# One operand tile of the FFN's seven-product loop placed 64 bytes further on

## The chip, the cores and the metric

The kernel runs on one core of one Trainium2 chip. The metric is the device time of one execution in microseconds (us): the median over runs.

## The reference, cut to what matters

Two layers of a streaming encoder over 512 positions of 1024 channels. Each layer has a mixing half (three attention-like branches, merged and projected) and a feed-forward half. The change lies in the feed-forward half:

```python
u = rms_norm(x, g_ffn[l]) * (1 + sc_f) + sh_f
h = jax.nn.silu(u @ w_ffn_gate[l]) * (u @ w_ffn_up[l])
x = x + gt_f * (h @ w_ffn_down[l])
```

The hidden width is 2816, that is 22 blocks of 128 hidden channels, in each of two layers.

## The kernel before, in words

Activations are held transposed: 128 channels on the partitions, 512 positions along the free dimension. Every float32 product is made of three fp32r matmuls (`mm3`, lines 225 to 227): with a matrix split into a high part and a low remainder, high times high (L225), weights high times activations low (L226), weights low times activations high (L227). In a matmul of the trace, `y<-t4h,wh` means: into `y`, moving operand (activations) `t4h`, stationary operand (weights) `wh`.

In the feed-forward half, the first three hidden blocks are computed plainly. For the other 19, gate and up are the two rows of a 2x2 block product over (half of the 1024 channels) x (half of the 512 positions), made with seven half-size products instead of eight. Four sums of weights are made for each block (`sums`: DVE L1011, POOL L1012 and L1013; `s31` and `s24` hold two each) and split by ACT and DVE (L269, L270); four differences of activations are made once for each layer and split by `divided` (lines 960 to 970: `t1` to `t4`, each a high and a low tile of 128 x 4 x 256 fp32r). Each product is four channel blocks times three matmuls, 12 matmuls of 256 columns.

The order on TensorE is as written in the loop over `f`. In one round, seen from the third product, TensorE does:

| product | into | weights | activations |
|---|---|---|---|
| t3 | y of block f | s31, first half | t3 |
| v | v of block f | s24, second half | uh/ul (the input itself) |
| z | z of block f+1 | a12 | uh/ul |
| t4 | y of block f | wh/wl, second half | t4 |
| t2 | y of block f+1 | s24, first half | t2 |
| t1 | v of block f+1 | s31, second half | t1 |
| y-u | y of block f+2 | wh/wl, first half | uh/ul |

After t2, ACT copies the half-made `y` out of PSUM (`kept_copy`, L1031), and t3 may not add to that bank before the copy is done. ACT's order around it is: cast of `s24h`, copy of `y` behind t2, copy of `v` behind t1, copy of the next `y`. The tiles `s31h`, `s31l` have one buffer: their next contents are cast (ACT L269) once t3, their last reader, has read them. Each engine runs its instructions in the program's order.

Where the tiles lie in a partition, as an offset into a line of 128 bytes: `uh`, `ul`, `wh`, `wl` and `t1` to `t4` begin at 0; `a12`, `s31` and `s24` begin at 64, since the pool that holds them ends with a tile of 16 floats (`half`, line 1092) and grows downwards from the pool of `t1` to `t4`. Of the seven products, y-u and t4 have both operands at 0; the other five have activations at 0 and weights at 64.

Of the kernel before, what the change touches and what calls it, by code (L numbers as in the profile page):

```python
# [8 lines left out]
F32 = mybir.dt.float32  # L9
# [8 lines left out]
P = 128  # L18
# [50 lines left out]
def tile_hybrid_trunk(ctx: ExitStack, tc: tile.TileContext, xT, cvec, pos, cst, cmask, vec, gfin,  # L69
# [14 lines left out]
    def scoped(name, side=None):  # L84
        return tc.tile_pool(name=name, bufs=1, side=side, reuse_waits="tile")
# [3 lines left out]
    def pst(tag, name):  # L89
        return ps.tile([P, S], F32, tag=tag, bufs=PB[tag], name=name)  # L90
# [112 lines left out]
    def W(unit, n=1, raw=3, ready=2, lag=0):  # L203

        i = at[0]
        if fourth[0]:
            raw, ready = 4, 3
        assert LOADS[i][0] == unit, (LOADS[i][0], unit)
        at[0] = i + n
        divide(i + n)  # L210

        def ahead():
            divide(i + max(n, ready + 1))
            fetch(i + max(n, raw + 1))

        if lag:
            later(lag, ahead)
        else:
            ahead()
        return splits[i] if n == 1 else splits[i : i + n]  # L220
# [8 lines left out]
    def gemm(o, wt, acts, m=P, start=True, stop=True, c0=0, cols=FULL):  # L229

        wh, wl = wt
        n = len(acts)
        for k, (ah, al) in enumerate(acts):
            cs = slice(c0 + k * m, c0 + (k + 1) * m)
            mm3(o, wh[:, cs], wl[:, cs], ah[:, cols], al[:, cols], start and k == 0, stop and k == n - 1)
            if k < n - 1:
                yield
# [25 lines left out]
    def run(g):  # L263
        for _ in g:
            tick()

    def split(h, l, src, scale=None):
        if scale is None:
            act.copy(h, src)  # L269
            dve.tensor_sub(l, src, h.bitcast(F32))  # L270
        else:
            act.activation(h, src, AF.Copy, scale=scale)
            dve.scalar_tensor_tensor(l, src, scale, h.bitcast(F32), ALU.mult, ALU.subtract)
# [240 lines left out]
    for l in range(L):  # L514
# [396 lines left out]
        tp = tp_.enter_context(scoped(f"st{l}", "right"))  # L911
# [16 lines left out]
        def gated(f, t, t2):  # L928
            g = tp.tile([P, S], F32, tag="g", bufs=3, name="g")
            fn(g, t, AF.Silu)  # L930
            dve.tensor_mul(g, g, t2)
            kept(f, g)
# [25 lines left out]
        def divided(name, src):  # L958
            h, lo = (tp.tile([P, 4, H], F32R, name=f"{name}{a}") for a in "hl")
            split(h, lo, src)  # L960
            TB[name] = [(h[:, k], lo[:, k]) for k in range(4)]
# [5 lines left out]
        pool.tensor_sub(b12, b22, b12)  # L967
        divided("t3", b12)
        dve.scalar_tensor_tensor(b21, b11, -1.0, b21, ALU.mult, ALU.subtract)
        divided("t4", b21)  # L970
        for f in range(1, NSTD):
            if f == 1:
                t = ts[2]
            else:
                t = pst("mm", "fg")
                run(gemm(t, W(("gu", l, 2 * f)), us))
            t2 = pst("s", "fu")
            run(gemm(t2, W(("gu", l, 2 * f + 1)), us))
            gated(f, t, t2)
# [281 lines left out]
def _build(arrays):  # L1261
    import concourse.bacc as bacc

    nc = bacc.Bacc("TRN2", target_bir_lowering=False, num_devices=1)
    feeds, args = {}, []
    for name, a in arrays.items():
        feeds[f"in_{name}_dram"] = a
        args.append(nc.dram_tensor(f"in_{name}_dram", a.shape, mybir.dt.from_np(a.dtype), kind="ExternalInput").ap())
    args.append(nc.dram_tensor("out_dram", (KC, P, S), F32, kind="ExternalOutput").ap())
    with tile.TileContext(nc) as tc:  # L1270
        tile_hybrid_trunk(tc, *args)
    return nc, feeds
# [10 lines left out]
```

## Time and profile before

| | |
|---|---|
| median of 3 runs | 1820.93 us (1818.77 to 1822.38) |
| the profiled execution's own time | 1820.55 us |
| its span (first to last instruction) | 1818.8 us |
| PE busy | 1783.5 us, 98% of the span |
| DVE busy | 1390.3 us, 76% |
| ACT busy | 956.8 us, 53% |
| mean granted TensorE clock | 0.997 of full speed |

PE is TensorE's matmuls, PEld its weight loads, which run beside the matmuls. Matmuls are pipelined, so the recorded length of one (0.28 us) is longer than the step from one start to the next; how long a product holds TensorE is read from the start of its first matmul to the start of the next product's first. In rows of the timeline the columns are: start in us from the span's start, length in us, engine, line, operation, out<-in, shape, count, and in brackets the idle time before it and what ended it.

### The profile page before, as it was taken

The page shows a single profiled execution, that of the slowest core. Times are in us where ns is not written, and L with a number is a line of the kernel's source. Part 1 is how long each engine was busy: PE and PEld are TensorE (multiplying, and loading weights), DVE is VectorE, ACT ScalarE, POOL GpSimd, SP SyncE. Part 2 cuts the span into 40 slices and gives each one's busy share as a digit, 9 for nine tenths or more (in the row PEclk, how much of TensorE's full clock was granted, in tenths as well). Part 3 has the DMA queues.
Part 4 walks back from the last instruction along what each step waited for, and adds up shares of the span by engine and source line. Part 5 has one row for each costly group of instructions (what it writes and reads, how often), then busy time and mean ns, then how long its engine had stood idle before and what let it go on. Part 6 is the DMA issues. An engine that isn't in the chain of part 4 may idle for free.

```text
span 1818.8 us, 27810 instructions
## 1 busy us (share of the span) xinstructions
PE 1783.5 (98%) x10324; PEld 1547.5 (85%) x10324; DVE 1390.3 (76%) x2317; ACT 956.8 (53%) x1735; POOL 258.9 (14%) x390
## 2 busy tenths in 40 slices
PE   8999999999999999999999999999999999999997
PEld 6788788888889899988887887888888889999887
DVE  8889887777668888967558898877776588898533
ACT  5667874453436555552257688645443374555531
POOL 0212100001000333300003121000110013232000
PEclk9999999999999999999999999999999999999999
DMA  8423324334654444468634223333365434445631
GB/s 338 110 67 85 88 76 122 121 113 133 214 162 151 129 133 145 128 218 272 209 119 103 61 69 88 104 122 115 117 201 171 149 93 122 140 136 163 215 96 46
DMA packets 86263, 247.52 MB, mean 136 GB/s; under 512 B 11824, under 2 KB 15024, under 8 KB 86128
## 3 DMA queue, kind: packets, MB, share of 16 engines
q1 hardware_dynamic: 75120, 224.83, 40.1%
q0 software_dynamic: 11008, 20.92, 4.0%
q8 instruction: 81, 1.33, 0.3%
q14 instruction: 54, 0.44, 0.1%
HBM read 220.74 MB, written 15.73 MB: 130 GB/s over the span
## 4 chain that ended last, share of the span: by engine, by line
PE 83%; DVE 7%; ACT 4%; issue 3%; DMA 2%; POOL 1%; DVEq 0%; SPq 0%; POOLq 0%; ACTq 0%
PE gate L225 5%; PE gate L227 5%; PE gate L226 5%; PE proj L225 5%; PE proj L226 4%; PE dn L226 4%; PE dn L227 4%; PE dn L225 4%; PE proj L227 4%; PE y L225 3%; PE y L227 3%; PE y L226 3%; PE o L225 2%; PE o L227 2%; PE o L226 2%
## 5 line engine op out<-in xcount | busy, mean ns | idle before, releaser
L196 ACT CAST wh<-wraw 128x1024 fp32r<-128x1024 f32 (+4 forms) x316 | 294.1, 934 | 312.4 <-PE dn L226 76.6
L198 DVE TENSOR_TENSOR wl<-wraw,wh 128x1024 fp32r<-128x1024 f32 (+4 forms) x316 | 361.1, 1146 | 116.1 <-ACT wh L196 110.2
L225 PE MATMUL proj<-uh,wh 128*128 128x512 f32 x384 | 161.1, 419 | 0.2
L225 PE MATMUL gate<-uh,wh 128*128 128x512 f32 x384 | 153.4, 400 | 0.0
L226 PE MATMUL proj<-ul,wh 128*128 128x512 f32 x384 | 151.2, 394 | 0.0
L227 PE MATMUL proj<-uh,wl 128*128 128x512 f32 x384 | 151.1, 393 | 0.0
L227 PE MATMUL gate<-uh,wl 128*128 128x512 f32 x384 | 150.2, 391 | 0.0
L226 PE MATMUL gate<-ul,wh 128*128 128x512 f32 x384 | 150.2, 391 | 0.0
L225 PE MATMUL dn<-wh 128*128 128x512 f32 (+1 forms) x396 | 145.1, 366 | 0.0
L226 PE MATMUL dn<-wl,wh 128*128 128x512 f32 (+1 forms) x396 | 144.9, 366 | 0.0
L227 PE MATMUL dn<-wh,wl 128*128 128x512 f32 (+1 forms) x396 | 144.7, 365 | 0.0
L395 DVE CUSTOM_DVE_ANT_0 wraw<-wraw,condb 128x1024 f32<-128x1024 f32 x80 | 97.6, 1220 | 56.9 <-DMA wraw<-in_w_ada_dram 56.7
L227 PEld LDWEIGHTS proj<-uh,wl 128*128 128x128 f32 x384 | 72.3, 188 | 16.7
L226 PEld LDWEIGHTS dn<-wl,wh 128*128 128x128 f32 x396 | 74.7, 189 | 12.8 <-DVE wl L198 0.7
L227 PEld LDWEIGHTS gate<-uh,wl 128*128 128x128 f32 x384 | 72.1, 188 | 15.8
L225 PEld LDWEIGHTS dn<-wh 128*128 128x128 f32 x396 | 74.7, 189 | 12.1
L227 PEld LDWEIGHTS dn<-wh,wl 128*128 128x128 f32 x396 | 74.7, 189 | 11.9
L225 PEld LDWEIGHTS gate<-uh,wh 128*128 128x128 f32 x384 | 72.2, 188 | 12.9
L1012 POOL TENSOR_TENSOR s<-s,wraw 128x512 f32<-128x512 f32 x38 | 49.2, 1295 | 239.0 <-ACT a12h L269 209.7
L226 PEld LDWEIGHTS gate<-ul,wh 128*128 128x128 f32 x384 | 72.3, 188 | 12.5
L106 ACT ACTIVATE lefts<-ss 128x512 f32<-128x512 f32 (+1 forms) x64 | 28.0, 438 | 100.0 <-DVE ss L446 84.4
L225 PEld LDWEIGHTS proj<-uh,wh 128*128 128x128 f32 x384 | 72.6, 189 | 9.0 <-PE sm L742 0.8
(440 smaller groups left out, 5314.7 us busy)
## 6 DMA issues: line engine op xcount, KB each, us to landing
wraw<-in_w_proj_dram SPq DMA_DIRECT2D x96, 512.0 KB, 3.8
wraw<-in_w_gu_dram SPq DMA_DIRECT2D x88, 512.0 KB, 4.2
wraw<-in_w_ada_dram SPq DMA_DIRECT2D x80, 512.0 KB, 3.6
wraw<-in_w_dn_dram SPq DMA_DIRECT2D x32, 512.0 KB, 4.0
wraw<-in_w_o_dram SPq DMA_DIRECT2D x48, 256.0 KB, 2.6
h_kept<-g POOLq DMA_DIRECT2D x44, 256.0 KB, 5.1
wraw<-h_kept SPq DMA_DIRECT2D x22, 512.0 KB, 5.0
wada<-in_w_ada_dram SPq DMA_DIRECT2D x16, 512.0 KB, 6.0
```

The costliest lines, as they stand in the source:

```text
L106: i = act.activation(*args, **kw).ins
L196: ins = [act.copy(wh[:, :c], raws[j][:, :c]).ins]
L198: ins.append(dve.tensor_sub(wl[:, :c], raws[j][:, :c], wh[:, :c].bitcast(F32)).ins)
L225: pe.matmul(o, wh, ah, start=start, stop=False, skip_group_check=again)
L226: pe.matmul(o, wh, al, start=False, stop=False, skip_group_check=again)
L227: pe.matmul(o, wl, ah, start=False, stop=stop, skip_group_check=again)
L395: ins = dve.tensor_tensor_reduce(out=wt, in0=wt, in1=condb, op0=ALU.mult, op1=ALU.add, scale=1.0, scalar=0.0, accum_out=m).ins
L1012: pool.tensor_add(s24[:, 0], s31[:, 1], ra[:, :HC])
```

## The change

Two tiles that nothing reads or writes are allocated around the fourth difference: 64 bytes before it and 192 bytes behind, in the pool that holds `t1` to `t4`.

```diff
         divided("t3", b12)
         dve.scalar_tensor_tensor(b21, b11, -1.0, b21, ALU.mult, ALU.subtract)
+        tp.tile([P, 16], F32, name="half0")
         divided("t4", b21)
+        tp.tile([P, 48], F32, name="half1")
         for f in range(1, NSTD):
```

No instruction is added, and on each engine they stand in the order of before; only addresses move. Of the seven products' operands (byte in the partition, and offset in a line of 128):

| tile | before | after |
|---|---|---|
| t3h | 212736 (0) | 212480 (0) |
| t4h | 220928 (0) | 220736 (64) |
| t4l | 225024 (0) | 224832 (64) |
| s31h | 177856 (64) | 177600 (64) |
| wh, three buffers in turn | 77056, 81152, 85248 (0) | the same |
| uh of the first channel block | 27904 (0) | the same |

The whole right-hand stack of the feed-forward half (`uf`, `g`, `t1` to `t3`, and `a12`, `s31`, `s24`, the copies) moves down by 256 bytes, which leaves its offset in a line as it was. In the table of products, t4 is the only row whose operands' distance changes: activations at 64, weights at 0. A few later instructions wait for one semaphore more, since a tile that follows there now overlaps another old one: of those on ACT, in each layer one cast of a kept h block waits for the second-last store of h besides the last.

## Rows read from the trace of the kernel before

**Rows 1.** The page: busy time by engine, and the engines' shares of the chain that ended last.
```profile
PE 1783.5 (98%) x10324; PEld 1547.5 (85%) x10324; DVE 1390.3 (76%) x2317; ACT 956.8 (53%) x1735; POOL 258.9 (14%) x390
...
PE 83%; DVE 7%; ACT 4%; issue 3%; DMA 2%; POOL 1%; DVEq 0%; SPq 0%; POOLq 0%; ACTq 0%
```
**Rows 2.** Groups of PE instructions, shapes kept apart: busy us, mean ns of one, idle before. One group of each kind of product (152 matmuls = 38 rounds x 4).
```profile
L225 PE MATMUL y<-uh,wh 128*128 128x256 f32 x152 | 43.0, 283 | 0.0
...
L225 PE MATMUL y<-t4h,wh 128*128 128x256 f32 x152 | 42.9, 282 | 0.0
L225 PE MATMUL y<-t3h,s31h 128*128 128x256 f32 x152 | 42.8, 282 | 5.2 <-ACT y L1031 5.0
L225 PE MATMUL z<-uh,a12h 128*128 128x256 f32 x152 | 42.3, 278 | 0.0
...
L225 PE MATMUL v<-t1h,s31h 128*128 128x256 f32 x152 | 42.0, 276 | 0.0
```
**Rows 3.** Timeline of PE in the middle of the first layer's loop: the first matmul of each product, over two rounds (from t3 to t3 to t3).
```profile
636.36 0.28 PE L225 MATMUL y<-t3h,s31h 128*128 128x256 f32 x1
...
637.76 0.28 PE L225 MATMUL v<-uh,s24h 128*128 128x256 f32 x1
...
639.18 0.28 PE L225 MATMUL z<-uh,a12h 128*128 128x256 f32 x1
...
640.59 0.28 PE L225 MATMUL y<-t4h,wh 128*128 128x256 f32 x1
...
642.02 0.28 PE L225 MATMUL y<-t2h,s24h 128*128 128x256 f32 x1
...
643.38 0.28 PE L225 MATMUL v<-t1h,s31h 128*128 128x256 f32 x1
...
644.74 0.28 PE L225 MATMUL y<-uh,wh 128*128 128x256 f32 x1
...
646.18 0.28 PE L225 MATMUL y<-t3h,s31h 128*128 128x256 f32 x1
...
647.54 0.28 PE L225 MATMUL v<-uh,s24h 128*128 128x256 f32 x1
...
648.90 0.28 PE L225 MATMUL z<-uh,a12h 128*128 128x256 f32 x1
...
650.26 0.28 PE L225 MATMUL y<-t4h,wh 128*128 128x256 f32 x1
...
651.70 0.28 PE L225 MATMUL y<-t2h,s24h 128*128 128x256 f32 x1
...
653.06 0.28 PE L225 MATMUL v<-t1h,s31h 128*128 128x256 f32 x1
...
654.42 0.28 PE L225 MATMUL y<-uh,wh 128*128 128x256 f32 x1
...
655.86 0.28 PE L225 MATMUL y<-t3h,s31h 128*128 128x256 f32 x1
```
**Rows 4.** Timeline of PE at the start of the same loop (the products t2, t1 and y-u, and the loop's first t3), and its last t3 but one.
```profile
609.85 0.30 PE L225 MATMUL y<-t2h,s24h 128*128 128x256 f32 x1
...
611.29 0.28 PE L225 MATMUL v<-t1h,s31h 128*128 128x256 f32 x1
...
612.70 0.28 PE L225 MATMUL y<-uh,wh 128*128 128x256 f32 x1
...
616.74 0.39 PE L225 MATMUL y<-t3h,s31h 128*128 128x256 f32 x1 [2.43 <-ACT y L1031]
...
783.07 0.39 PE L225 MATMUL y<-t3h,s31h 128*128 128x256 f32 x1 [0.19 <-ACT y L1031]
```
**Rows 5.** Timeline of all engines in the second of the two rounds of rows 3: the work on the weights' sums and the copy that t3 waits for.
```profile
645.54 0.36 ACT L1031 COPY y<-y 128x256 f32<-128x256 f32 x1
...
647.32 0.28 PE L226 MATMUL y<-t3l,s31h 128*128 128x256 f32 x1
...
647.68 1.05 ACT L269 CAST s31h<-s 128x1024 fp32r<-128x1024 f32 x1 [0.89 <-PE y L226]
...
648.77 1.22 DVE L270 TENSOR_TENSOR s31l<-s,s31h 128x1024 fp32r<-128x1024 f32 x1 [0.54 <-ACT s31h L269]
...
649.91 0.42 DVE L1083 TENSOR_TENSOR g<-v,y 128x256 f32<-128x256 f32 x1
...
650.36 0.63 ACT L106 ACTIVATE g<-g 128x512 f32<-128x512 f32 x1 [1.62 <-DVE g L1083]
...
650.90 0.61 ACT L269 CAST a12h<-wraw 128x512 fp32r<-128x512 f32 x1
...
651.61 1.29 POOL L1012 TENSOR_TENSOR s<-s,wraw 128x512 f32<-128x512 f32 x1 [6.55 <-ACT a12h L269]
...
652.98 1.37 POOL L1013 TENSOR_TENSOR s<-s,wraw 128x512 f32<-128x512 f32 x1
...
654.38 1.05 ACT L269 CAST s24h<-s 128x1024 fp32r<-128x1024 f32 x1 [1.55 <-POOL s L1013]
655.34 0.36 ACT L1031 COPY y<-y 128x256 f32<-128x256 f32 x1
```
**Rows 6.** Timeline of PE at the end of the same loop: the last t1, then the last t3 (no y-u stands between them there), the last t4 and the first matmul behind the loop.
```profile
790.21 0.28 PE L225 MATMUL v<-t1h,s31h 128*128 128x256 f32 x1
...
791.57 0.28 PE L225 MATMUL y<-t3h,s31h 128*128 128x256 f32 x1
...
794.29 0.28 PE L225 MATMUL y<-t4h,wh 128*128 128x256 f32 x1
...
795.73 0.40 PE L225 MATMUL dn<-wh 128*128 128x512 f32 x1
```

## The prediction, made before the changed kernel ran

> **What bounds the kernel now.** First the page's busy times and its chain: TensorE is busy for 98% of the span and holds 83% of the chain that ended last [rows 1]. So a step saved between matmuls counts, unless TensorE then waits for somebody. Next the groups by shape: in the loop of seven products the matmuls with both operands at offset 0 have a recorded mean of 283 and 282 ns, those 64 bytes apart 276, 278 or 282 [rows 2]. Recorded lengths of pipelined matmuls overlap, so the price is read from the starts in the timeline [rows 3], product by product, 12 matmuls each. The reader is to see three paces there:
>
> - y-u and t4, operands at the same offset: 1.44 us in the second round (644.74 to 646.18, and 650.26 to 651.70), 0.120 us a matmul.
> - Products 64 bytes apart, fast: 1.36 us, 0.113 a matmul (t2, t1 in both rounds; t3, v, z in the second).
> - The same products, slow: 1.41 us, 0.118 a matmul (t3, v, z in the first round, 636.36 to 640.59: 4.23 for three).
>
> So 64 bytes of distance alone do not give the fast pace. The two rounds alternate: one takes 646.18 - 636.36 = 9.82, the next 655.86 - 646.18 = 9.68 us [rows 3]. What sets the slow pace is the third view, t3's start against the copy that it waits for [rows 5]. In the fast round's start the copy of y ends at 645.54 + 0.36 = 645.90 and t3 starts 0.28 later; in the next it ends at 655.34 + 0.36 = 655.70 and t3 starts 0.16 later. The nearer of the two is the released one: t3 came late by a hair, and in the loop's first rounds, where it came late by 2.43 us [rows 4], it is slow as well. I read it so: **a product that starts late runs at 0.118, and so do all products 64 bytes apart behind it, until a product at equal offsets (y-u or t4) has passed; behind that, unless late, they run at 0.113.** In the first round of rows 3, z is slow, then t4 passes, then t2 and t1 are fast. At the loop's start a slight wait shows in t2's first matmul, 0.30 us instead of 0.28; t2 takes 1.44, and t1 behind it stays slow at 1.41 [rows 4].
>
> Why t3 is late every second round shows in the same rows: a ring of work that runs beside TensorE. t3's last reader of s31h starts at 647.32 and frees the only buffer; then in order the cast of s31h (647.68), its remainder on DVE (648.77), g (649.91), silu (650.36), the cast of a12h (650.90), two sums on POOL (651.61, 652.98), the cast of s24h (654.38), the copy of y (655.34), and t3 again at 655.86 [rows 5]. From t3 to t3 this ring takes 9.68 us, and in a fast round TensorE's own work is 5 x 1.36 + 2 x 1.44 = 9.68 as well. They are tied; none of the ring's steps waits for t4.
>
> **The change, part by part.** Two tiles without users cost nothing: no instruction is issued for them. The extra semaphores hang on stores of h that left long before the last one, which is waited for anyway; I cost them at nothing. The 256 bytes by which the neighbours move leave every other distance as it was. What is left is t4, 12 matmuls in each of 38 rounds.
>
> 1. *t4 itself.* Its bounds by the nearest rows: 1.36 at the fast pace, 1.41 at the slow, 1.44 or 1.43 as now (650.26 to 651.70; 640.59 to 642.02) [rows 3]; no product that starts on time takes more than 1.44, so I put no loss on t4 alone. In a fast round I take 1.36, a gain of 0.08; in a slow one 1.41, a gain of 0.02. TensorE alone would give 38 x 0.05, about 2 us, or 3 at best.
> 2. *The ring takes the fast rounds' gain.* TensorE's work falls to 6 x 1.36 + 1.44 = 9.60, the ring stays at 9.68. So t3 waits 0.08 longer: the round stays at 9.68, gain 0, and t3 is late in every such round, hence slow.
> 3. *The slow rounds lose t4 as the passage that restores the pace.* With t4 64 bytes apart from its weights, nothing stands between z and t2, so t2 and t1 run slow too, up to y-u: 6 x 1.41 + 1.44 = 9.90 against 9.82 now, a loss of 0.08. The ring, which gets 0.05 longer with t3, is at 9.73 and does not end last; t3 is on time and the next round is fast.
> 4. *Count.* From the loop's first t3 at 616.74 to the last but one at 783.07 [rows 4] are 17 rounds in 166.33 us: 17 x 9.68 = 164.6, so 1.7 over, of which some 0.3 is the further wait before 783.07 and the rest 9 slow rounds at 0.15. Loss 9 x 0.08 = 0.7 a loop. That last wait can hide one of them. At the end no y-u follows t1, which goes straight into the last t3 [rows 6]: t2, t1, t3 and v would be slow, 4 x 0.05, and two t4 gain 0.02 each: +0.15. Together 0.8 a loop, 1.6 in two layers.
>
> **Sum:** the profiled execution's 1820.55 + 1.6 = 1822.2; that execution stands 0.4 below the median of the runs shown, so **1822.5 us** against 1820.93, +0.09%. About 0.2% (3.6 us) is what a measurement of this kernel can tell from no change: the three runs lie 3.6 us apart. So I forecast no change that can be told.
>
> **The rivals.**
>
> *t4 still restores the pace, or breaks it* (25%). At t4's edges there is one load of weights at the offset that the matmul before it reads: wh at 0 under the last of z (uh at 0), s24h at 64 under the last of t4 (64). If one such meeting does what 12 do now, t2 and t1 are fast again, slow rounds take 9.80, and the loops gain 9 x 0.02 + 0.1 = 0.3 each: 1820.3. If it instead makes t4, t2 and t1 slow in all rounds, every round takes 3 x 1.36 + 3 x 1.41 + 1.44 = 9.75, on time for the ring, and the mean of before (9.75) is kept: 1820.9. For it: the pace now ends wherever equal offsets meet. Against: that takes 12 matmuls in every row, one meeting alone stands in none, and in the first round of rows 3 the slow pace goes through two changes of operands, t3 to v to z, unharmed.
>
> *The distance is not what t4 feels* (12%). All the fast products have weights at 64, none has activations at 64; if the weights' own place is what counts, t4 stays at 1.44 and the time at 1820.9. [...]
>
> *The slow pace holds in all rounds* (10%, the side that loses). If the 12 matmuls of y-u cannot restore the pace once it has been carried from t3 through t4 to t1, every round takes 6 x 1.41 + 1.44 = 9.90, never waits for the ring, and nothing ends it. Against a mean of 9.75 that is 0.15 x 17 + 0.2 a loop, +5.5 in all: 1826.4, +0.3%. It decides as soon as a round whose t3 was on time is slow. Against it: t4 with as many matmuls restores the pace now [rows 3].
>
> *The late start does no harm, or the ring gives way* (11%). If all rounds run at the ring's 9.68, the slow ones gain 0.15 x 9 + 0.3 a loop: 1817.6. If the ring moves with t4 after all, and rounds take 9.60, it is 1814.7, -0.34%. For it, only that I take the ring from releasers that a trace infers; against it, both rounds fit to 0.01 us.
>
> **How the numbers follow.** Forecast 42%, the rivals 25, 12, 10 and 11. The range takes in the forecast, the first two rivals and the run-to-run spread around them, and leaves most of the last two out: 1818.4 to 1824.6. Faster by over 0.2%: the 1814.7 case and part of the 1817.6 one, 6%. Slower: the third rival and a part of the spread, 10%. Same: 84%.
>
> **What would show it.** Right: t4's group mean falls from 282 to between 276 and 280, alternating rounds of 9.68 and 9.90 with t4 at 1.36 and 1.41, t2 and t1 at 1.41 in every second round, and PE's waits for ACT's copy of y in many small pieces. Wrong: t4 still at 1.44 (the second rival); t2 and t1 fast in all rounds (the first); t3 slow where its copy ended over 0.2 us before (the third); rounds under 9.68 (the fourth).

## The result, and the profile after

The changed kernel takes 1827.24 us against 1822.68 for the kernel before on the same chip (medians of 16 runs each): a ratio of 1.0028, interval 1.0020 to 1.0036. It is slower by 4.6 us, a little more than can be told from no change, and outside the range of the prediction. One of the changed kernel's 16 runs took 3340.34 us at a granted clock of 0.533, and the ratio leaves it out. The profiled span is 1822.6 us against 1818.8.

The first view is the groups of PE instructions in the profile of the changed kernel (busy us, mean ns of one, idle before; behind the two added lines of code, line numbers are two higher than in the kernel before: L1033 is L1031 there):

```profile
L225 PE MATMUL y<-t3h,s31h 128*128 128x256 f32 x152 | 42.9, 282 | 4.9 <-ACT y L1033 4.9
L225 PE MATMUL y<-uh,wh 128*128 128x256 f32 x152 | 42.9, 282 | 0.0
...
L225 PE MATMUL y<-t4h,wh 128*128 128x256 f32 x152 | 42.5, 280 | 0.0
...
L225 PE MATMUL v<-t1h,s31h 128*128 128x256 f32 x152 | 42.4, 279 | 0.0
...
L225 PE MATMUL z<-uh,a12h 128*128 128x256 f32 x152 | 42.4, 279 | 0.0
```

They answer to [rows 2]: t4 fell from 282 to 280, as far as forecast; but v with t1 rose from 276 to 279 and z from 278 to 279. So something spread to products whose operands kept their distance. The wait for ACT's copy of y in front of t3 is 4.9 us where it was 5.0. All of it stands before the first t3 of the two loops (2.43 and 2.46 us), and not in the many small pieces that were forecast.

Where the pace went stands in the timeline of PE in the changed kernel, the first matmul of each product from one y-u to the next and on to t3:

```profile
643.31 0.28 PE L225 MATMUL y<-uh,wh 128*128 128x256 f32 x1
...
644.75 0.28 PE L225 MATMUL y<-t3h,s31h 128*128 128x256 f32 x1
...
646.17 0.28 PE L225 MATMUL v<-uh,s24h 128*128 128x256 f32 x1
...
647.58 0.28 PE L225 MATMUL z<-uh,a12h 128*128 128x256 f32 x1
...
648.99 0.28 PE L225 MATMUL y<-t4h,wh 128*128 128x256 f32 x1
...
650.40 0.28 PE L225 MATMUL y<-t2h,s24h 128*128 128x256 f32 x1
...
651.82 0.28 PE L225 MATMUL v<-t1h,s31h 128*128 128x256 f32 x1
...
653.23 0.28 PE L225 MATMUL y<-uh,wh 128*128 128x256 f32 x1
...
654.67 0.28 PE L225 MATMUL y<-t3h,s31h 128*128 128x256 f32 x1
```

And the copy of y that this t3 at 644.75 waits for, in the timeline of ACT of the same kernel:

```profile
644.04 0.36 ACT L1033 COPY y<-y 128x256 f32<-128x256 f32 x1
```

Beside [rows 3]: six products take 1.41 to 1.42 and y-u 1.44, from t3 to t3 9.92 us, and the round that follows takes 9.92 again. There is no alternation any more. The copy had ended at 644.40, 0.35 before t3 started (the rows of before show 0.28 for a t3 on time, [rows 5]), and the product is slow all the same. That is what the third rival named as its sign. The granted clock is 1.00 in both rounds shown here and in both of [rows 3], so the pace is not the clock's.

In all, from the loop's first t3 to the end of its last t4, the two loops take 181.56 and 181.68 us; before they took 178.99 and 179.24. Between the two profiled executions that is +5.0 us, a little more than the whole of their difference (1824.36 against 1820.55).

### The profile page after: what moved, and what is told of

It reads as the page before. It is cut to its first block, busy times and chain, and to the rows that moved or that the text cites. A ratio compares the mean times of both kernels' runs of the same rounds, so it can differ in the third digit from the quotient of the medians.

```text
span 1822.6 us, 27811 instructions
## 1 busy us (share of the span) xinstructions
PE 1787.5 (98%) x10324; PEld 1552.0 (85%) x10324; DVE 1389.9 (76%) x2317; ACT 957.6 (53%) x1735; POOL 259.1 (14%) x390
## 4 chain that ended last, share of the span: by engine, by line
PE 79%; DVE 8%; DMA 5%; ACT 4%; issue 3%; POOL 1%; DVEq 0%; SPq 0%; ACTq 0%; POOLq 0%
PE gate L225 5%; PE gate L227 5%; PE gate L226 5%; PE proj L225 5%; PE proj L226 4%; PE proj L227 4%; PE y L225 4%; PE y L226 4%; PE y L227 4%; DMA wraw<-in_w_ada_dram 3%; PE o L225 2%; PE o L227 2%; PE o L226 2%; PE dn L227 2%; PE dn L226 2%
```

## The experiments

In the expectations, theory A says that the slow pace is passed on from round to round with nothing late, B that the distance within 512 bytes matters, C that t3 is late in every round; the later letters are explained where they stand. "Copy first" below means ACT's copy of y behind t2 ordered ahead of the next cast of `s24h`. The table is worked out from each kernel's timeline as above: us of a product in the rounds in the middle of the loop, the round from t3 to t3, both loops, and the ratio to the kernel before. Two values with a stroke between them are those of rounds that alternate. One execution of each kernel is traced, and the rounds and loops are that one's; the ratio is from all its runs.

| kernel | t3, v, z | t4 | t2, t1 | y-u | round | loops | ratio (95%) |
|---|---|---|---|---|---|---|---|
| before | 1.36 / 1.41 | 1.44 / 1.43 | 1.36 | 1.44 | 9.68 / 9.83 | 178.99, 179.24 | 1 |
| changed | 1.41 | 1.41 | 1.42, 1.41 | 1.44 | 9.92 | 181.56, 181.68 | 1.0028 (1.0020 to 1.0036) |
| x1_shift | 1.36 / 1.41 | 1.44 / 1.43 | 1.36 | 1.44 | 9.68 / 9.83 | 179.07, 180.77 | 1.0003 (0.9993 to 1.0014) |
| x2_512 | 1.41 | 1.41 | 1.42, 1.41 | 1.44 | 9.92 | 181.57, 181.67 | 1.0027 (1.0015 to 1.0038) |
| x3_high | 1.36 | 1.42 | 1.41 | 1.43 | 9.75 | 179.07, 181.19 | 1.0000 (0.9989 to 1.0012) |
| x4_ring_before | 1.36 | 1.44 | 1.36 | 1.44 | 9.68 | 177.11, 176.96 | 1.0019 (1.0007 to 1.0031) |
| x5_ring_after | 1.41 | 1.41 | 1.42, 1.41 | 1.44 | 9.92 | 181.36, 181.36 | 1.0027 (1.0012 to 1.0041) |
| x8_copy_before | 1.36 | 1.44 | 1.36 | 1.44 | 9.68 | 177.93, 177.91 | 0.9951 (0.9938 to 0.9965) |
| x9_copy_after | 1.41 | 1.41 | 1.42, 1.41 | 1.44 | 9.92 | 182.17, 182.15 | 0.9980 (0.9970 to 0.9990) |
| x12_one | 1.36 / 1.41 | 1.37 / 1.41 | 1.41 | 1.44 / 1.43 | 9.83 / 10.03 | 182.12, 182.12 | 0.9995 (0.9986 to 1.0004) |
| x13_two | 1.36 | 1.37 | 1.41 | 1.43 | 9.94 | 182.25, 182.25 | 1.0002 (0.9993 to 1.0011) |
| x14_one_first | 1.36 | 1.37 | 1.41 | 1.43 | 9.70 | 178.44, 178.43 | 0.9966 (0.9952 to 0.9979) |
| x15_weights | 1.41, 1.37, 1.36 | 1.41 | 1.41 | 1.37 | 9.75 | 178.79, 178.79 | 0.9988 (0.9979 to 0.9997) |
| x17_t4_minus | 1.36 | 1.42 | 1.42, 1.41 | 1.43 | 9.76 | 180.37, 180.69 | 1.0003 (0.9992 to 1.0013) |
| x18_t4_minus_copy | 1.36 | 1.42 | 1.42, 1.41 | 1.43 | 9.76 | 179.41, 179.25 | 0.9963 (0.9948 to 0.9977) |
| x16_all_minus | 1.36 | 1.36 | 1.36 | 1.36 | 9.52 | 175.30, 175.08 | 0.9953 (0.9935 to 0.9972) |
| x20_seam | 1.36 | 1.36 | 1.41 | 1.43 | 9.82 | 180.56, 180.56 | 0.9982 (0.9972 to 0.9991) |
| x21_seam_first | 1.36 | 1.36 | 1.41 | 1.43 | 9.82 | 181.91, 180.59 | 0.9985 (0.9975 to 0.9994) |

Four of these loops (the second of x1_shift and of x3_high, both of x17_t4_minus) hold something else. Behind the wait of 2.4 us before their first t3 the granted clock falls to 0.50 for some 3 us, in which matmuls start 213 ns apart, and the first round takes about 1.5 us more (11.58 us against 10.05 in the other loop of x1_shift). These are to be compared by their later rounds.

**Is it the distance, or the 256 bytes by which the neighbours move?** x1_shift moves the stack as the change does and leaves t4 at offset 0; x2_512 moves it by 512 bytes with t4 64 bytes on.

```diff
x1_shift, against the change:
-        tp.tile([P, 16], F32, name="half0")
         divided("t4", b21)
-        tp.tile([P, 48], F32, name="half1")
+        tp.tile([P, 64], F32, name="half1")
x2_512, against the change:
-        tp.tile([P, 48], F32, name="half1")
+        tp.tile([P, 112], F32, name="half1")
```

> All four differences at offset 0 as before, and the right-hand stack 256 bytes lower as in the change. Theory A (the slow pace of 0.118 us a matmul passes through every product whose operands are 64 bytes apart, y-u does not end it, t4 at equal offsets does): rounds alternate between 9.68 and 9.82 us as before, time of before within 0.1%. Theory B (the 256 bytes are to blame: distances that are now 256 or 320 bytes in a line of 512 no longer end the slow pace): rounds of 9.8 to 9.95 throughout, t2 and t1 at 1.41 us, +0.15 to +0.3%.

> The change with 448 bytes behind t4 in place of 192: t4 stays at offset 64, and the stack moves by 512 bytes in place of 256. Theory A: as the changed kernel, all rounds 9.92 us, +0.28% against before. Theory B: y-u ends the slow pace again, rounds alternate between 9.68 and 9.90, about +0.1%.

x1_shift alternates as before and costs nothing that can be told; x2_512 is the changed kernel again. So t4's 64 bytes are the cause, and neither the shift nor the distance within 512 bytes is.

**Half of the edit.** x3_high places only `t4h` 64 bytes on, so that every third matmul of t4 still meets its weights at equal offsets.

```diff
...
+            if apart:
+                tp.tile([P, 16], F32, name="half0")
+            h = tp.tile([P, 4, H], F32R, name=f"{name}h")
+            if apart:
+                tp.tile([P, 48], F32, name="half1")
+            lo = tp.tile([P, 4, H], F32R, name=f"{name}l")
...
-        divided("t4", b21)
+        divided("t4", b21, True)
```

> The change on t4's high tile alone: t4h at offset 64, t4l at 0, so that 8 of t4's 12 matmuls are 64 bytes apart and 4 (every third) at equal offsets. If a single matmul at equal offsets can end the slow pace, t2 and t1 are fast again and rounds alternate, time of before within 0.1%. Theory A with a run of such matmuls needed: slow throughout, 9.9 to 9.95 us a round, +0.3%.

Neither expectation came. Behind the first, nearly every round is the same 9.75, with t2 and t1 slow and y-u *ending* the slow pace. So y-u can end it, and in the changed kernel it doesn't.

**Is t3 late in each round?** x4_ring_before and x5_ring_after give the sums `s31` a second pair of buffers, which cuts the ring; the room for it comes from loading the second pair of kept blocks after the loop.

```diff
-            h, lo = (gs.tile([P, D], F32R, tag=nm_ + a, bufs=1 + i, name=nm_ + a) for a in "hl")
+            h, lo = (gs.tile([P, D], F32R, tag=nm_ + a, bufs=2, name=nm_ + a) for a in "hl")
...
-                cap[0] = first_of["h", l, 2]
+                cap[0] = first_of["h", l, 1]
```

> The kernel before with two buffers for the halves of s31 in place of one (the room comes from loading the second pair of kept h blocks behind the loop in place of before its end): the cast of s31h no longer waits for t3, so the ring is cut. Theory A and the theory of the ring (C: late starts make slow rounds): after the first round no t3 is late, t4 ends the slow pace once, then every round takes 9.68 us with all products 64 bytes apart at 1.36; 16 slow rounds gain 0.15 each, -2.4 us, -0.13%. If the alternation has another cause than the late t3, it stays and the time is that of before.

> The changed kernel with the ring cut in the same way. Theory A: the first t3 of each loop still starts late, the slow pace is then passed on for ever, rounds of 9.92 us, time of the changed kernel (+0.28% against before). Theory C (the slow pace needs a late t3 in each round to live): after the first round all are fast, 6 x 1.36 + 1.44 = 9.60 us, 37 x 0.15 to 0.2 us under before, -0.3%.

Two starts of t3 in x4_ring_before, in the timeline of PE:

```profile
645.61 0.28 PE L225 MATMUL y<-t3h,s31h 128*128 128x256 f32 x1
...
655.29 0.28 PE L225 MATMUL y<-t3h,s31h 128*128 128x256 f32 x1
```

and the copy of y that the second of them waits for, on ACT in the same kernel:

```profile
652.74 0.38 ACT L1031 COPY y<-y 128x256 f32<-128x256 f32 x1 [0.48 <-PE y L227]
```

The copy ends 2.17 us before t3; with the ring cut no t3 is late, the alternation is gone, and from the second round on all take the fast 9.68. The loops are 2 us shorter each, and yet the whole is 0.2% longer, where 0.13% less was expected. A part of that is the way to the loops' first t3: it starts 11.2 and 11.3 us after the loop's first product instead of 9.7, since t2 and t1 run at a granted clock of 0.50 for a while behind a wait of 2.5 us. Where the rest stands was not followed. The changed kernel with the same cut stays at 9.92 with no late t3, not even the first, which theory A had expected late: the slow pace stands before it. So the ring made the late starts of before, and in the changed kernel nothing has to be late: the slow pace hands itself on.

**The same with one order on ACT.** x8_copy_before and x9_copy_after leave the buffers and order the copy of y ahead of the cast.

```diff
+            if after:
+                tc.add_manual_dep(c, after.name, order, reason="the copy first")
...
-                summed(f + 1, 1)
...
+            if f + 1 < NF:
+                summed(f + 1, 1, kept_ins["y2"])
```

> The kernel before with ACT's copy of y (behind t2) ahead of the cast of the next s24h in place of behind it; same buffers. Both theories: the ring from t3 to t3 no longer passes through t3's wait, so t3 is never late, the loop's first wait of 2.4 us goes too, and t4 at equal offsets ends a slow pace within a round: all rounds 9.68 us. 2 x 2.4 + 17 x 0.15 = about -7 us, -0.4%. If something else feeds the alternation, rounds still alternate and only the 2 x 2.4 go, -0.25%.

> The changed kernel with the same order on ACT. Theory A (a pace is passed on, whichever it is, and y-u does not end the slow one): all rounds of a loop alike, 9.92 us if the loop begins slow (a slight wait in its first t2 makes that the likelier), which is 2 x 2.4 us less and 2 x 18 x 0.15 more than before, +0.1%; 9.60 if it begins fast, -0.5%. Theory C (each late t3 makes its own slow round): no t3 is late, so 9.60 us from the second round on, -0.5%.

Two starts of t3 in x8_copy_before:

```profile
642.96 0.28 PE L225 MATMUL y<-t3h,s31h 128*128 128x256 f32 x1
...
652.64 0.28 PE L225 MATMUL y<-t3h,s31h 128*128 128x256 f32 x1
```

and in x9_copy_after:

```profile
654.73 0.28 PE L225 MATMUL y<-t3h,s31h 128*128 128x256 f32 x1
...
664.65 0.28 PE L225 MATMUL y<-t3h,s31h 128*128 128x256 f32 x1
```

9.68 against 9.92 in every round behind the first: with no late t3 the change costs 4.2 us a loop in the traced executions. A late start is left in each loop of both kernels, v in the first round. In the first loop of x9_copy_after t3 still runs at 113 ns before it, and every product 64 bytes apart behind it is slow, to the loop's end. The medians of the whole runs lie 4.8 us apart (1819.09 and 1814.25), not 8.5, and x9_copy_after is 0.2% faster than before where 0.1% slower was expected. Its traced execution is the slowest of its twelve (1822.84), so whether the loops of the others all ran at this pace is open. x8_copy_before, 1814.25 us, beats both kernels.

A late start does not always begin the slow pace. The late v and the z behind it in the first and in the second loop of x8_copy_before, in the timeline of PE:

```profile
615.17 0.38 PE L225 MATMUL v<-uh,s24h 128*128 128x256 f32 x1 [0.52 <-ACT v L1036]
...
616.64 0.28 PE L225 MATMUL z<-uh,a12h 128*128 128x256 f32 x1
...
1503.89 0.39 PE L225 MATMUL v<-uh,s24h 128*128 128x256 f32 x1 [0.58 <-ACT v L1036]
...
1505.41 0.28 PE L225 MATMUL z<-uh,a12h 128*128 128x256 f32 x1
```

In the first loop t3 before the wait runs at 118 ns a matmul and v behind it at 113 (1.47 us with the late start in it); in the second it is the other way round, 113 before and 118 behind (1.52).

**Why does y-u not end it?** Three kernels on the base of x9_copy_after put one or two more matmuls ahead of y-u, in each round or (x14_one_first, whose lines are shown) only in the first two.

```diff
+            if f < NSTD + 2:
+                for _ in range(1):
+                    pe.matmul(spare_, half(SW[f, 0], 1)[3][1], TB["t1"][3][0], start=True, stop=True)
```

> The changed kernel with ACT's copy of y put ahead of the next cast (so that no t3 of the loop after the first is late), and one more matmul in each round ahead of y-u: weights s31l, activations t1h, 64 bytes apart, into a PSUM bank that nothing reads. It costs some 0.11 to 0.12 us a round. Theory E (whether y-u ends the slow pace hangs on the step of the pace's cycle at which it is entered, and one matmul shifts that step): y-u is entered one step later, settles as it did in the kernel before, and the products behind it take 1.36: rounds of 6 x 1.36 + 1.44 + 0.11 = 9.71, against 9.92 without the extra matmul; the loops gain 17 x 0.2 x 2, about 7 us, time 0.9945 of before. Theory F (with t4 64 bytes apart y-u never ends it, at whatever step): t3 to t1 stay at 1.41, rounds of 9.92 + 0.12 = 10.04, 4 us more than without it: 1.0000 of before.

> The same with two more matmuls ahead of y-u in each round, s31l by t1h, 64 bytes apart. Theory E: a second shift of the step; if the step after the second one is also one from which y-u settles, products of 1.36 and rounds of 9.60 + 0.23 = 9.83, time about 0.997 of before; if not, 9.92 + 0.24 = 10.16. Theory F: 10.16 in any case, time about 1.002 of before. One of the two kernels with one and two extra matmuls may differ from the other under E, never under F.

> The same with one more matmul ahead of y-u in the first two rounds of each loop alone. Theory E: once y-u has ended the slow pace and no t3 is late, t4 64 bytes apart keeps the fast one: rounds of 6 x 1.36 + 1.44 = 9.60 for the rest of the loop, below the 9.68 of the kernel before with the same order on ACT; time about 0.9935 of before, if the ring of sums lets rounds be 9.60. Theory F: 9.92 throughout, 0.998 of before.

The timeline of PE in x14_one_first, a round long after the extra matmuls:

```profile
652.90 0.28 PE L225 MATMUL y<-t3h,s31h 128*128 128x256 f32 x1
...
654.26 0.28 PE L225 MATMUL v<-uh,s24h 128*128 128x256 f32 x1
...
655.62 0.28 PE L225 MATMUL z<-uh,a12h 128*128 128x256 f32 x1
...
656.98 0.28 PE L225 MATMUL y<-t4h,wh 128*128 128x256 f32 x1
...
658.34 0.28 PE L225 MATMUL y<-t2h,s24h 128*128 128x256 f32 x1
...
659.76 0.28 PE L225 MATMUL v<-t1h,s31h 128*128 128x256 f32 x1
...
661.17 0.28 PE L225 MATMUL y<-uh,wh 128*128 128x256 f32 x1
...
662.60 0.28 PE L225 MATMUL y<-t3h,s31h 128*128 128x256 f32 x1
```

This is the case's clearest row of evidence. From the third round on x14_one_first and x9_copy_after issue the same instructions with the same addresses, and one takes 9.70 a round to the loop's end, the other 9.92. In the rounds compared the granted clock is 1.00 in both. They ran on different chips, but x12_one has y-u ending the slow pace and not ending it in turn within one execution. So one kernel's pace is carried on from round to round at 9.70 and the other's at 9.92, and one matmul more in each of the first two rounds decided it. The whole runs show less of it: their medians are 1816.93 and 1819.09 us, with ratios whose intervals overlap (table), where the two loops together are 7.4 us apart and the traced executions 8.5 (1814.34 and 1822.84). What pace the loops of the other executions ran at isn't known. Theory F falls. Theory E holds in that one matmul changes what y-u does, not in its sizes: it put t2 and t1 at 1.36, and they are slow in every round, so no round reaches 9.60. With one extra matmul in each round, y-u ends the slow pace in every second round only (9.83, 10.03), with two in each.

The steps behind it, in ns from one start to the next, 12 to a product, worked out from the starts in the traces:

```
y-u, x9_copy_after:     121 120 124 118 117 121 120 124 118 117 121 122   then t3 at 118
y-u, x14_one_first:     117 118 119 121 117 117 121 119 120 120 120 121   then t3 at 113
t4 behind a slow z, before: 118 120 120 117 118 120 120 120 120 120 120 120   then t2 at 113
t4, x14_one_first:      115 113 114 113 113 114 114 112 114 114 112 118   then t2 at 118
```

In these runs a product at equal offsets that settles to a steady 120 leaves the fast pace behind it; one that goes round in a cycle of five (121, 120, 124, 118, 117) doesn't. From the y-u ahead of a loop's first t3 on, in the loops of all traced executions, 168 y-u and t4 at equal offsets go round in the cycle (two or three of their steps take 123 to 126 ns; none of the other 560 has such a step), and the product behind each of the 168 is slow. Behind the others the next product of the loop is fast, but for 48 t3 that start 0.17 us or less after the copy that they wait for has ended. Which of the two it does hangs on how it is entered: one more matmul ahead of it in two rounds changed it in x14_one_first. In x1_shift's first round t4 itself, at equal offsets, goes round in that cycle, and t2 and t1 behind it are slow.

**Does a common distance help?** x15_weights leaves t4 where it was and moves the weights' tiles by 64 bytes, so that all seven products are 64 bytes apart. Taken within 256 bytes, t1 to t4 then lie 64 behind their weights, and uh 64 before them. x17_t4_minus and x18_t4_minus_copy mirror the change (t4 64 before its weights). x16_all_minus moves t1 to t4 and the sums as well, so that in all seven products the activations lie 64 before the weights.

```diff
x15_weights, against x8_copy_before:
-    end_.tile([P, 56], F32, name="end")
+    end_.tile([P, 24], F32, name="end")
...
+                wp.tile([P, 16], F32, tag="w0", bufs=1, name="w0")
...
+                wp.tile([P, 16], F32, tag="w1", bufs=1, name="w1")
x16_all_minus, against x15_weights:
         divided("t4", b21)
+        tp.tile([P, 32], F32, name="pad")
...
-        gs.tile([P, 16], F32, name="half")
+        gs.tile([P, 48], F32, name="half")
x17_t4_minus, against the change (x18_t4_minus_copy with the copy first too):
-        tp.tile([P, 16], F32, name="half0")
+        tp.tile([P, 48], F32, name="half0")
         divided("t4", b21)
-        tp.tile([P, 48], F32, name="half1")
+        tp.tile([P, 16], F32, name="half1")
```

> The kernel before (t4 at offset 0) with ACT's copy of y put first, and instead of t4 the weights' tiles wh and wl begin 64 bytes into a line (64 bytes before and 64 behind them, taken from the 224 unused bytes at the stack's other end, so every other tile keeps its offset). In the loop all seven products are then 64 bytes apart, all weights at 64 and all activations at 0: no load of weights lies at the offset of the activations that the matmul before it reads. Outside the loop the weights' distance changes too, which I can't price. Theory G (a product's own distance sets 0.113 or 0.120 a matmul; a slow pace begins at a late start, or where the load meets the offset being read, and ends only in a product at equal offsets): the loop's first t3 is late, no product at equal offsets follows, so all rounds take 7 x 1.41 = 9.87 to 9.9, some 0.2 x 17 x 2 = 7 us more than with t4 and y-u at equal offsets: 0.999 of before. Theory H (the slow pace ends by itself where nothing meets): 7 x 1.36 = 9.52 a round, unless the ring of sums holds it at 9.6 to 9.68: up to 5 us less than that kernel, 0.992 of before. If the loop's times are as in either and the whole is not, the rest lies in the other stages.

> The change mirrored: 192 bytes ahead of the fourth difference and 64 behind, so t4 lies 64 bytes before its weights' offset in 256 (192 against 0) where the change has it 64 behind (64 against 0). Everything else lies as in the changed kernel. Theory S (the sign counts: activations 64 bytes behind their weights have two paces that keep themselves up, 0.113 and 0.118; 64 bytes before them they run at 0.113 and end the slow pace): t4 takes 1.36 and t2, t1 behind it 1.36, in rounds with a late t3 3 x 1.41 + 3 x 1.36 + 1.44 = 9.75 and in others at least the ring's 9.68: 1817 to 1820, 0.997 to 0.9985 of before. Theory D (only the distance within a line of 128 counts): as the change, 9.92 in all rounds, 1.0028.

> The same with ACT's copy of y put first, so that no t3 behind the first is late. Theory S: rounds of 6 x 1.36 + 1.44 = 9.60 if the ring lets them be so short, 9.68 if not: 0.9935 to 0.995 of before. Theory D: 9.92, 0.998 of before.

> The kernel with the weights' tiles moved by 64 bytes, with the tiles t1 to t4 and the weights' sums moved so that in all seven products the activations lie 64 bytes before their weights. Theory S: all products at 1.36, rounds of 9.52, or 9.6 to 9.68 if the ring of sums ends last; against 9.75 with four products on the other side, 0.07 to 0.23 x 17 x 2 = 2.4 to 7.8 us less than that kernel's 1820.2: 0.9945 to 0.9975 of before. Theory D: the loop's first late t3 sets 1.41 for all, 9.87 a round: 1.001.

A round of x15_weights in the timeline of PE:

```profile
655.53 0.28 PE L229 MATMUL y<-t3h,s31h 128*128 128x256 f32 x1
...
656.94 0.28 PE L229 MATMUL v<-uh,s24h 128*128 128x256 f32 x1
...
658.31 0.28 PE L229 MATMUL z<-uh,a12h 128*128 128x256 f32 x1
...
659.67 0.28 PE L229 MATMUL y<-t4h,wh 128*128 128x256 f32 x1
...
661.08 0.28 PE L229 MATMUL y<-t2h,s24h 128*128 128x256 f32 x1
...
662.50 0.28 PE L229 MATMUL v<-t1h,s31h 128*128 128x256 f32 x1
...
663.91 0.28 PE L229 MATMUL y<-uh,wh 128*128 128x256 f32 x1
...
665.27 0.28 PE L229 MATMUL y<-t3h,s31h 128*128 128x256 f32 x1
```

The four products with t1 to t4 take 1.41, the three with uh 1.36 or 1.37, every round behind the first. Theories G and H both fall: y-u and v run fast straight behind slow products, with nothing at equal offsets between. That the two kinds differ, though both are 64 apart in a line of 128, is why I took the distance within 256 for the next runs. The whole is 6 us longer than that of x8_copy_before (medians), the loops together only 1.7: the first loop's first product begins 3.0 us later, so the moved weights seem to cost elsewhere too.

Of x18_t4_minus_copy, from z to t1:

```profile
657.74 0.28 PE L225 MATMUL z<-uh,a12h 128*128 128x256 f32 x1
...
659.10 0.28 PE L225 MATMUL y<-t4h,wh 128*128 128x256 f32 x1
...
660.51 0.28 PE L225 MATMUL y<-t2h,s24h 128*128 128x256 f32 x1
...
661.93 0.28 PE L225 MATMUL v<-t1h,s31h 128*128 128x256 f32 x1
```

t4 on the other side takes 1.42 right behind a fast z, and t2 and t1 follow it at 1.42 and 1.41. So that side is not fast by itself; theory S falls in x17 and x18 as a whole (9.76, not 9.60 to 9.75), and D too (not 9.92). Half of S has rows on its side, though. Behind a slow z, t4 on the other side takes 1.37 or 1.38 and ends the slow pace in six of the seven rounds of x17 and x18 that hold one, as in the last round of the first loop of x17_t4_minus, from z to t1:

```profile
786.12 0.28 PE L225 MATMUL z<-uh,a12h 128*128 128x256 f32 x1
...
787.53 0.28 PE L225 MATMUL y<-t4h,wh 128*128 128x256 f32 x1
...
788.90 0.28 PE L225 MATMUL y<-t2h,s24h 128*128 128x256 f32 x1
...
790.26 0.28 PE L225 MATMUL v<-t1h,s31h 128*128 128x256 f32 x1
```

Of x16_all_minus, from t3 to t3:

```profile
654.46 0.28 PE L229 MATMUL y<-t3h,s31h 128*128 128x256 f32 x1
...
658.54 0.28 PE L229 MATMUL y<-t4h,wh 128*128 128x256 f32 x1
...
659.90 0.28 PE L229 MATMUL y<-t2h,s24h 128*128 128x256 f32 x1
...
663.98 0.28 PE L229 MATMUL y<-t3h,s31h 128*128 128x256 f32 x1
```

Seven products at 1.36, 9.52 a round, as S had it. But S's reason isn't shown by it: with one distance in all products no change of distance is left either, which may be the reason as well, and one common distance on the other side, which would tell the two apart, was not tried. Nor does that side shed a slow pace by itself: in the first loop z, t2, t1, y-u and t3 run at 118 ns a matmul, and only the late start of v behind them ends it (222, 118, 122, 116, 114, 113). The whole, 1813.65 us, is level with x8_copy_before, whose order on ACT it has too: the loops give 5.5 us (175.3 and 175.1 against 177.9 each), and about as much is lost outside them, a part of it before the first loop, whose first product begins 2.7 us later.

**What starts it in a fast round?** x20_seam and x21_seam_first put one matmul with activations and weights at offset 0 between t4 and t2, so that the weights of t2 load beside that matmul and not beside t4's last (in the trace of the changed kernel the load of t2's first weights and t4's last matmul both start at 650.29; in that of x21_seam_first the load and the extra matmul both start at 660.27).

```diff
             product(y_, half(RA[f], 1), TB["t4"], False)
+            if f + 1 < NF:
+                pe.matmul(spare_, half(RA[f], 1)[3][1], B[0, 0][3][0], start=True, stop=True)
```

> The changed kernel with ACT's copy of y put first, and one more matmul in each round between t4 and t2: wl of t4's last channel block by uh at offset 0, into a bank that nothing reads. While t4's last matmul reads activations at 64 (of 256), the weights loaded beside it now lie at 0 and not at 192 (s24h); while the extra one reads at 0, those loaded lie at 192, as everywhere in the loop. Theory M (the slow pace begins at the one meeting of t4's activations and s24h's load): in rounds that begin fast, t2 and t1 take 1.36: 6 x 1.36 + 1.44 + 0.11 = 9.71. Whether y-u ends the first slow pace is open here: if it never does, 10.04. Theory N (t4's own 12 matmuls, or the change of distance, start it): t2 and t1 at 1.41 in every round: 9.70 + 0.12 = 9.82 at best.

> The same, with one more matmul ahead of y-u in the first two rounds of each loop, which was enough to make the rounds behind it begin fast. Theory M: t2, t1 and all others at 1.36 from the third round on: 9.71 a round. Theory N: t2 and t1 at 1.41, 9.82 a round.

The seam in x21_seam_first:

```profile
658.91 0.28 PE L225 MATMUL y<-t4h,wh 128*128 128x256 f32 x1
...
660.27 0.28 PE L1101 MATMUL spare<-uh,wl 128*128 128x256 f32 x1
660.39 0.28 PE L225 MATMUL y<-t2h,s24h 128*128 128x256 f32 x1
...
661.80 0.28 PE L225 MATMUL v<-t1h,s31h 128*128 128x256 f32 x1
```

t4 is fast here, 1.36, with no long step at its end, and t2 is slow all the same: theory M falls as put, and N gives the right time (9.82). But N's reason isn't shown either, since the extra matmul took 0.12 itself. What x14 and x21 share is one step of 118 or 120 ns after a row at 113; in both the slow pace starts right behind it. I take one step that is 5 to 7 ns too long as the trigger; no run removes it without putting another in its place, so that stays argued. The length of a step alone can't be it: t4 in the kernel before takes twelve steps of 119 to 121 behind a fast z, and t2 behind them is fast.

## Why the prediction was wrong, point by point

- **What bounds the kernel**: right. TensorE is the bound (PE is busy for 98% of the changed kernel's span as well), the ring ties with the fast round at 9.68 and makes t3 late every second round: x4_ring_before and x8_copy_before remove the late start, and the alternation goes.
- **t4 itself**: 1.36 and 1.41 were forecast, 1.41 came in every round; x14_one_first shows 1.37. The term is right for the pace that it meets.
- **The step that failed** is the rule in the first part: products 64 bytes apart stay slow "until a product at equal offsets (y-u or t4) has passed; behind that, unless late, they run at 0.113". For y-u in the changed kernel it is false: it passes in each round, t3 is on time (0.35 us behind the end of its copy), and t3 is slow (1.41 us), round after round of 9.92. From that, step 3's "t3 is on time and the next round is fast" fell, and with it the alternation of 9.68 and 9.90. The rows had shown t4 doing it from one way of being entered ([rows 3], behind a slow z), and I took it as a property of the product. x9_copy_after against x14_one_first shows that it isn't: the same y-u ends the slow pace in one and not in the other, by how it is entered. The trace of before held a sign of it: y-u behind the slow t1 at the loop's start goes round in the cycle there (120, 120, 125, 117, 118, 120, 120, 125), and only the late t3 behind it, slow in any case, hid what it leads to. The rule's first words are too wide as well: v starts late in the first loop of x8_copy_before and runs at 113.
- **Step 2**, the ring takes the fast rounds' gain: never came to bear, since no fast round arose.
- **The third rival** (10%) happened, by its mechanism and its price: 9.90 a round forecast, 9.92 measured; +5.5 us for the loops, +5.0 measured; 1.003 forecast, 1.0028 measured. What I held against it, that "t4 with as many matmuls restores the pace now", says nothing about y-u entered otherwise. It deserved more than one chance in ten: one restored pace in the rows shown, that behind t4 in the first round of [rows 3], was all that stood against it.
- **The first rival's second half** (t4's edges make t4, t2 and t1 slow in all rounds, 9.75) is close to what happens where the rounds are kept fast: 9.70 in x14_one_first, since t4 takes 1.37 there. So with no late t3 the change had nothing to gain in either state: 9.70 or 9.92 against 9.68 for x8_copy_before.
- **The second rival** (the distance isn't what t4 feels) fell with t4's 1.41. That addresses count shows in a whole round too: x16_all_minus and x8_copy_before run the same products at 9.52 and 9.68 with only addresses moved between them.

## What to carry to other kernels

Where pipelined matmuls follow each other without a gap, read their starts, not their lengths (here 0.28 us at 113 and at 118 ns a matmul alike), and in more than one round: a pace can be handed on from product to product (9.70 and 9.92 us a round for the same instructions), and a round's time then says as much about how it was entered as about what it holds. Moving one operand of a cycle changes the seams on both sides of it, and these were dearer here (t2 and t1 together 0.11 us a round) than the product's own gain (0.02 to 0.03); giving all of them one distance shortened the round (x16_all_minus, 9.52) but not the whole, and what paid in the whole was taking away the late start (x8_copy_before, one order on ACT, 0.5%). When a rule read from one round carries the forecast, price its failure at more than a tenth.

## What the runs showed of the hardware that was not expected

- The same instructions at the same addresses keep up either of two times a round for a whole loop, 9.70 and 9.92 us (x14_one_first, x9_copy_after), at a mean granted clock of 0.995 and 0.996.
- Twelve matmuls of 256 columns take 1.36, 1.41 or 1.44 us by the offsets of their operands and by what ran before, a spread of 6%.
- A late start can end the slow pace as well as begin it: v behind a wait of 0.52 us in the first loop of x8_copy_before goes from 118 to 113 ns a matmul, behind one of 0.58 in its second loop from 113 to 118 (x16_all_minus, v in the first loop, as the first).
